# Front of an encoder kernel: S5 vectors loaded first, dummy products, squares after the input, first state products one projection later, one tile pool for three phases

## The chip, the cores and the metric

The kernel runs on one NeuronCore of a Trainium2 chip, in one launch. The metric is the device time of one execution in microseconds (us), from which three runs of the kernel before are shown below; the profiled execution is a further one.

## The reference

A trunk of two layers over 512 positions of width 1024, all in fp32. What matters here is layer 0, whose first stage is changed most:

```
h = rms_norm(x, g)                               # over the 1024 features
z = h @ w_in                                     # 1024 x 2048: q, k, v, u (512 columns each)
a = neighbourhood_attention(q, k, v, rpb)        # 8 heads of 64
lam_bar = exp(lam * exp(log_dt))                 # S5: 2 directions, 32 groups, 64 complex states
b_bar   = ((lam_bar - 1) / lam) * B
state_t = lam_bar * state_(t-1) + b_bar @ u_t    # forwards and backwards
y = u * d + sum over directions of Re(C @ state)
x = x + concat(a, glu(gelu(y))) @ w_out
```

After it, in both layers, come a gated MLP with a convolution of width 3 over the positions ("ffn", 2816 hidden features, two halves), a gated per-layer input ("ple"), and in layer 1 a retention mixer in place of the above; a last RMSNorm ends it.

## The kernel before

**Tiles.** Positions lie on the free axis: a tile is 128 features x 512 positions, and x is eight such tiles. Every projection (`proj`, L139 to L143 with `mm3`) makes 128 output features: eight weight blocks of 128x128, each with three matmuls of 128x512, since a number is carried as a rounded high part and a low rest: low weights x high x (L141), high x high (L142), high weights x low x (L143). That is 24 matmuls a projection in layer 0. `split` makes the two parts of x (high on ScalarE L177, low on VectorE L178).

**Weights.** They come in chunks c0, c1, c2 ... of eight blocks, in the order of use: chunks c0 to c3 are the four u projections, c4 to c7 are q0 to q3, c8 to c11 are k0 to k3. SyncE (SP) fetches a chunk into `wr` (three buffers), ScalarE rounds it to `wh` (L113), and VectorE subtracts to `wl` (L121, from c4 on L123). For chunks c6 to c15 `wl` is -`wr` on ScalarE (L118), onto which a DMA issued by GpSimd (POOL) adds the weights again from HBM (L119). `wh` and `wl` have four buffers each, so a chunk's split waits until the projection four before it has read its own.

**Stage one** (`mixer0`). On ScalarE and VectorE the order up to `region.close()` is that of the code; on TensorE (PE) and elsewhere a scheduler places what the code writes. `prep_small` queues the small S5 vectors (dt, magnitude, angle, powers of lam_bar: 128x32 and the like) as a list, from which `do(n)` emits n at a time between the splits of x; they read `svec`. Each x tile is also squared (L209) and the squares are added to one tile on VectorE; four products with a column of ones (L241, in `Rstd`) sum it over the partitions, and POOL and VectorE make r = 1/rms of it (128x4). `spread` turns r into a row over all partitions with four PE transposes (L252) and a ScalarE copy (L255).

The projections of u and q need no r; what reads them multiplies by the row: `u_out` (L563) scales u on VectorE, writes it to HBM (`u_scr`, L566), and reads it back in another order as `U` (L567). The input tables of S5 are made by `prep_w1` for table q of eight (three VectorE operations for each of a real and an imaginary part, on p1r, p1i and the b tables, 128x512), and turned by `trans_w1` (four PE transposes each, L487, then a ScalarE copy L489). `states` multiplies a pair of tables with `U` (L591), and four pairs fill `XV`, on which the scans run (`local`, `carry`). `prep_w2` makes output tables, `prep_blk` zeroed tiles into which blocks of the b tables are copied, `strips0` a first product of b and c tables with which this stage of PE ends. The loop that ties them together (L676 to L692):

```
for n in range(8):
    prep_w1(n + 1)               # tables for the next step
    ps = proj(xg) if n else q0   # q0 to q3, then k0 to k3
    if n:
        after_trans(n - 1)       # turn table n - 1; after odd ones, states of the pair
    next_w2(W2_K[n])
```

**Later phases.** `tp` ("act") is a pool of 53 tiles of 128x512 for everything; in the ffn a second pool `fe` of 20 tiles, made anew for each ffn, takes some of the hidden layer's high and low parts (h, l), and in the retention one of 16 tiles (`rte`). They lie in space that the other phases use otherwise. In the ffn each of 22 steps makes two projections, two tiles `c` (L1008 on ScalarE, two VectorE operations each, then gelu, a product on POOL, high part on ScalarE L1018, low part on POOL).

## Time and profile before

| what | value |
|---|---|
| median of three runs | 1525.79 us (1525.31 to 1527.48) |
| profiled execution, its own time | 1527.03 us |
| its span, first to last instruction | 1525.2 us |
| mean granted TensorE clock in it | 0.991 |
| PE busy | 1495.3 us (98%) |
| VectorE (DVE) busy | 915.7 us (60%) |
| ScalarE (ACT) busy | 615.1 us (40%) |
| POOL busy | 363.9 us (24%) |

The profile's times count from the first instruction of the profiled execution; its own time is 1.8 us more than the span, and lies 1.24 us above the median. A granted clock of 1.00 is the full 2.4 GHz, 0.50 is 1.2 GHz. PE rows give a matmul's time with its overlap with the next, so what a matmul costs in a chain is the distance between two starts.

### The profile page before, as it was taken

Reading aid. Unit: us, or ns where it says so; the run is one execution under the profiler, and the core shown is the slowest. Engines: PE = TensorE matmul, PEld = TensorE weight load, DVE = VectorE, ACT = ScalarE, POOL = GpSimd, SP = SyncE. Lnnn points to the kernel's source line nnn. Section 1 sums busy time; section 2 is a strip of 40 time slices with the busy share of each in tenths; the row PEclk is TensorE's granted clock in tenths of the full one; section 3 lists DMA queues with packets and bytes.
Section 4 is the critical chain, followed back from the end, with each engine's and each line's share of the span. In section 5 each row is a group of like instructions: output and inputs, shape, how many; then the busy total and the mean of one; then the engine's idle time right before and its main releaser. Section 6 shows DMA issues by size and latency. Waiting matters only on the chain.

```text
span 1525.2 us, 18170 instructions
## 1 busy us (share of the span) xinstructions
PE 1495.3 (98%) x7152; PEld 1234.6 (81%) x7152; DVE 915.7 (60%) x1225; ACT 615.1 (40%) x859; POOL 363.9 (24%) x256
## 2 busy tenths in 40 slices
PE   7899999999999999999999999999999999999998
PEld 5687788888888888887888888888888888888887
DVE  8778966877676523485454544534467676743346
ACT  6344755544444322343434232422244444432233
POOL 0100001233232212063141231413122222212105
PEclk9799999999999999999999999999999999999999
DMA  5854392333333433333222222213333333333331
GB/s 198 219 111 141 102 255 61 94 107 97 98 96 98 120 93 93 120 126 108 72 70 84 68 84 69 83 56 97 97 97 97 97 97 97 97 97 96 97 125 56
DMA packets 58934, 158.95 MB, mean 104 GB/s; under 512 B 11744, under 2 KB 15968, under 8 KB 58848
## 3 DMA queue, kind: packets, MB, share of 16 engines
q1 hardware_dynamic: 57408, 152.55, 32.9%
q0 software_dynamic: 1440, 5.24, 2.1%
q8 instruction: 56, 0.92, 0.2%
q14 instruction: 30, 0.25, 0.1%
HBM read 149.94 MB, written 7.83 MB: 103 GB/s over the span
## 4 chain that ended last, share of the span: by engine, by line
PE 84%; DVE 7%; issue 6%; DMA 1%; POOL 1%; ACT 1%; SPq 0%; DVEq 0%; POOLq 0%; ACTq 0%
PE ps L141 27%; PE ps L143 27%; PE ps L142 27%; DVE t L168 4%; PE ps L591 1%; PE ps L926 1%; DMA t<-in_xp_dram 1%; DVE wl L123 1%; DVE t L277 1%; DVE t L774 0%; PE ps L816 0%; PE ps L241 0%; PE ps L487 0%; POOL t L175 0%; DMA vecs<-in_vec_dram 0%
## 5 line engine op out<-in xcount | busy, mean ns | idle before, releaser
L141 PE MATMUL ps<-t,wl 128*128 128x512 f32 x1568 | 615.9, 393 | 11.3 <-DVE wl L551 6.8
L142 PE MATMUL ps<-t,wh 128*128 128x512 f32 x1568 | 611.8, 390 | 0.0
L143 PE MATMUL ps<-t,wh 128*128 128x512 f32 x1568 | 608.8, 390 | 0.7 <-DVE t L277 0.7
L113 ACT ACTIVATE wh<-wr 128x1024 fp32r<-128x1024 f32 x241 | 254.4, 1059 | 556.2 <-PE ps L143 277.5
L123 DVE TENSOR_TENSOR wl<-wr,wh 128x1024 fp32r<-128x1024 f32 x228 | 298.2, 1309 | 288.9 <-ACT wh L113 288.8
L141 PEld LDWEIGHTS ps<-t,wl 128*128 128x128 f32 x1568 | 296.2, 189 | 75.5 <-DVE wl L551 6.8
L143 PEld LDWEIGHTS ps<-t,wh 128*128 128x128 f32 x1568 | 295.8, 189 | 64.2 <-DVE t L277 1.8
L142 PEld LDWEIGHTS ps<-t,wh 128*128 128x128 f32 x1568 | 296.3, 189 | 60.2
L168 POOL TENSOR_TENSOR t<-t,t 128x512 f32<-128x512 f32 x117 | 177.9, 1522 | 457.6 <-ACT t L1014 279.3
L168 DVE TENSOR_TENSOR t<-ps,t 128x512 f32<-128x512 f32 (+1 forms) x86 | 59.3, 698 | 114.8 <-PE ps L143 103.4
L168 DVE TENSOR_TENSOR t<-t,t 128x512 f32<-128x512 f32 (+2 forms) x113 | 96.8, 878 | 27.8 <-ACT t L200 20.7
L168 DVE TENSOR_TENSOR pad<-ps,t 128x512 f32<-128x512 f32 x88 | 60.5, 692 | 82.4 <-PE ps L143 82.4
L1010 DVE SCALAR_TENSOR_TENSOR t<-pad,vecs,t 128x512 f32<-128x512 f32 x88 | 102.3, 1164 | 1.4
L168 POOL TENSOR_TENSOR t<-t 128x512 f32<-128x512 f32 x33 | 50.3, 1527 | 190.0 <-DVE t L168 190.0
L141 PE MATMUL ps<-e,wl 128*128 128x512 f32 x216 | 85.4, 395 | 0.0
L143 PE MATMUL ps<-e,wh 128*128 128x512 f32 x216 | 85.3, 395 | 0.0
L142 PE MATMUL ps<-e,wh 128*128 128x512 f32 x216 | 85.2, 395 | 0.0
L175 POOL TENSOR_TENSOR t<-t,t 128x512 fp32r<-128x512 f32 x41 | 58.6, 1446 | 60.1 <-ACT t L174 51.5
L1011 DVE SCALAR_TENSOR_TENSOR t<-pad,vecs,t 128x512 f32<-128x512 f32 x88 | 70.0, 796 | 2.9
L1008 ACT ACTIVATE t<-pad,vecs 128x512 f32<-128x512 f32 x88 | 70.2, 802 | 3.4 <-DVE pad L168 3.4
L141 PE MATMUL ps<-wh,t 128*128 128x512 f32 x160 | 62.6, 391 | 0.0
L143 PE MATMUL ps<-wl,t 128*128 128x512 f32 x160 | 62.3, 389 | 0.0
(212 smaller groups left out, 1314.1 us busy)
## 6 DMA issues: line engine op xcount, KB each, us to landing
wr<-in_wts_dram SPq DMA_DIRECT2D x241, 512.0 KB, 3.6
wl<-in_wts_dram POOLq DMA_DIRECT2D x10, 512.0 KB, 7.5
pj_scr<-t SPq DMA_DIRECT2D x16, 256.0 KB, 5.1
t<-pj_scr SPq DMA_DIRECT2D x16, 256.0 KB, 4.1
t<-in_xp_dram SPq DMA_DIRECT2D x8, 256.0 KB, 5.3
t<-in_bias_dram SPq DMA_DIRECT2D x8, 256.0 KB, 4.1
Tm<-k_scr SPq DMA_DIRECT2D x8, 256.0 KB, 6.7
t<-in_xn_dram SPq DMA_DIRECT2D x8, 256.0 KB, 6.6
```

The costliest lines, as they stand in the source:

```text
L113: act.activation(out=h, in_=raw, func=ACTF.Copy)
L123: late.append(lambda: dve.tensor_tensor(out=l, in0=raw, in1=f(h), op=ALU.subtract))
L141: pe.matmul(out=ps, lhsT=lhs[1], rhs=rhs[0], start=start, stop=False)
L142: pe.matmul(out=ps, lhsT=lhs[0], rhs=rhs[0], start=False, stop=False)
L143: pe.matmul(out=ps, lhsT=lhs[0], rhs=rhs[1], start=False, stop=stop)
L168: eng.tensor_tensor(out=out, in0=a, in1=b, op=op)
L175: low.tensor_tensor(out=l, in0=src, in1=f(h), op=ALU.subtract)
L277: self.late.append(lambda: dve.scalar_tensor_tensor(out=l, in0=x, scalar=g, in1=f(h), op0=ALU.mult, op1=ALU.subtract))
L591: pe.matmul(out=pw[:, i, :], lhsT=w1t["ri"[c], g // 4][:, 128 * (g % 4):128 * (g % 4) + 128], rhs=U[:, g, :], start=True, stop=True)
L1008: act.activation(out=c, in_=t[:, 1:513], func=ACTF.Identity, scale=vcol(cw + 44 + j), bias=vcol(V_CB + 44 * i + j))
L1010: dve.scalar_tensor_tensor(out=c, in0=t[:, 0:512], scalar=vcol(cw + j), in1=c, op0=ALU.mult, op1=ALU.add)
L1011: dve.scalar_tensor_tensor(out=c, in0=t[:, 2:514], scalar=vcol(cw + 88 + j), in1=c, op0=ALU.mult, op1=ALU.add)
```

## The change

Seven edits, in the order in which they run:

- `svec` is the first DMA of SP, ahead of x; the first eight small vector operations stand ahead of the split of x0 (`DO_X`).
- Ten products of the ones tile with itself (128x128) stand on PE ahead of the first projection (`WARM`); nothing reads them.
- All eight splits of x come before the squares, and the weights of chunk c2 are split before them. The squares are added in pairs only, so `Rstd` sums four tiles with 16 products in place of one with four.
- Table 1 (`prep_w1(1)`) is made before r, and q1 is multiplied before `spread`.
- Tables are turned and multiplied two steps behind the projections in place of one (`after_trans(n - 2)`).
- The zeros of `prep_blk` are written by four ScalarE copies of the ones scaled by 0, not by POOL memsets.
- One pool "upper" of 20 tiles, opened past the first mixer and kept to the end, replaces the 20 of each ffn and the 16 of the retention. It takes x, the rms row, the tiles `c` and the low parts of the last seven hidden tiles; the rest of h and l, and all of the retention's, are in `tp`. The 8 tiles `full` of the last phase come from `tp` too.

```diff
-DO_X = (0, 0, 0, 6, 6, 6, 6, 6)
+DO_X = (8, 6, 4, 6, 6, 6, 6, 6)
+WARM = 10
+UPPER = 20
...
-            parts = ss.parts()
+            parts = ss if isinstance(ss, list) else ss.parts()
...
-            self.row = T()
+            self.row = T(special=True)
...
+        svec = sp.tile([128, 96], F32, name="svec")
+        nc.sync.dma_start(out=svec, in_=vec[:, V_LRE:V_LRE + 96])
         xt = [T() for _ in range(KD)]
...
-                    pool.memset(t, 0.0)
+                    act.activation(out=t.rearrange("p (a b) -> p a b", b=128),
+                                   in_=ones.rearrange("p (a b) -> p a b", a=1).to_broadcast([128, 4, 128]),
+                                   func=ACTF.Copy, scale=0.0)
...
+        wm = PS()
+        for _ in range(WARM):
+            pe.matmul(out=wm[:, 0:128], lhsT=ones, rhs=ones, start=True, stop=True)
         prep_small()
         for k in range(KD):
+            do(DO_X[k])
             xg.append(split(xt[k], scale=nvec[:, k:k + 1]))
-            do(DO_X[k])
...
-            if k >= SQ_LAG:
-                ss.add(xt[k - SQ_LAG], sq=True)
-        for k in range(KD - SQ_LAG, KD):
-            ss.add(xt[k], sq=True)
+        w_split(2)
+        squares = []
+
+        def square(k):
+            t = T()
+            act.activation(out=t, in_=xt[k], func=ACTF.Square)
+            if k % 2:
+                tt(dve, squares[-1], squares[-1], t, ALU.add)
+            else:
+                squares.append(t)
+
+        for k in range(4):
+            square(k)
...
         w_split(3)
+        for k in range(4, KD):
+            square(k)
         do(99)
...
-        st_ = Rstd(ss, D)
-        q0 = proj(xg)
+        prep_w1(1, "r")
+        prep_w1(1, "i")
+        st_ = Rstd(squares, D)
+        ready = [proj(xg), proj(xg)]
         st_.spread()
...
-            if n < 7:
-                prep_w1(n + 1, "r")
-                prep_w1(n + 1, "i")
+            if n < 6:
+                prep_w1(n + 2, "r")
+                prep_w1(n + 2, "i")
...
-            ps = proj(xg) if n else q0
+            ps = ready.pop(0) if ready else proj(xg)
...
-            if n:
-                after_trans(n - 1)
+            if n > 1:
+                after_trans(n - 2)
             next_w2(W2_K[n])
+        after_trans(6)
         after_trans(7)
...
+        upper[0] = ctx.enter_context(tc.tile_pool(name="upper", bufs=UPPER))
...
-        extra[0] = ph.enter_context(tc.tile_pool(name=f"fe{i}", bufs=20))
...
-                c = T()
+                c = T(special=True)
...
-            use = m < 10
-            h, l = T(F32R, special=use), T(F32R, special=use)
+            h, l = T(F32R), T(F32R, special=m >= KF - 7)
...
-        extra[0] = ph.enter_context(tc.tile_pool(name="rte", bufs=16))
...
-                    ys[4 * h + e] = split(sg[e], low=pool, special=4 * h + e < 7)
+                    ys[4 * h + e] = split(sg[e], low=pool, special=4 * h + e < 0)
```

On PE, between the sums of squares and the second pair of state products, the kernel before has these rows (the projections' rows, 24 for each of q0, q1 and q2, are left out; ps_552/ps_559 turn table 0, ps_630/ps_637 table 1):

```order
L241 MATMUL ps_426<-ones,t_163 128x1 x4
...
L252 MATMUL ps_471<-idn,r_431 128x128 x4
...
L487 MATMUL ps_552<-idn,t_352 128x128 x4
L487 MATMUL ps_559<-idn,t_388 128x128 x4
...
L487 MATMUL ps_630<-idn,t_496 128x128 x4
L487 MATMUL ps_637<-idn,t_501 128x128 x4
L591 MATMUL ps_644<-U,t_557 128x64 x4
L591 MATMUL ps_644<-U,t_635 128x64 x4
L591 MATMUL ps_655<-U,t_564 128x64 x4
L591 MATMUL ps_655<-U,t_642 128x64 x4
```

The changed kernel has these rows on PE from the end of the 16 sums on (left out are q0 and q1 ahead of the spread, q2 and q3 ahead of the turns, and k0 ahead of the last two rows, which turn table 2; t_434 and t_439 are table 1):

```order
L243 MATMUL ps_444<-ones,t_281 128x1
...
L254 MATMUL ps_533<-idn,r_461 128x128 x4
...
L491 MATMUL ps_646<-idn,t_360 128x128 x4
L491 MATMUL ps_653<-idn,t_396 128x128 x4
...
L491 MATMUL ps_704<-idn,t_434 128x128 x4
L491 MATMUL ps_711<-idn,t_439 128x128 x4
L610 MATMUL ps_718<-U,t_651 128x64 x4
L610 MATMUL ps_729<-U,t_658 128x64 x4
...
L491 MATMUL ps_789<-idn,t_558 128x128 x4
L491 MATMUL ps_796<-idn,t_563 128x128 x4
```

The spread has moved behind q1, and the first state products behind q3 in place of q2; only the products with table 0 stand there, those with table 1 follow behind k0.

On DVE, around the operation that reads the sums of squares (v), the kernel before makes table 1 behind the four scaled u (t_478 to t_490) and the sign change of a c table (t_118):

```order
L245 TENSOR_SCALAR v_432<-ps_426 128x4
L168 TENSOR_TENSOR v_432<-v_432,r_431 128x4 x2
...
L168 TENSOR_TENSOR t_478<-ps_287,t_476 128x512
...
L331 TENSOR_SCALAR t_118<-t_118 128x512
L168 TENSOR_TENSOR t_496<-p1r,t_312 128x512
...
L168 TENSOR_TENSOR t_496<-t_496,t_497 128x512
...
L168 TENSOR_TENSOR t_501<-t_501,t_502 128x512
```

The changed kernel has there (t_434 and t_439 are table 1, t_540 the first scaled u, t_118 the sign change, t_558 table 2):

```order
L170 TENSOR_TENSOR t_434<-p1r,t_320 128x512
L170 TENSOR_TENSOR t_435<-p1i,t_325 128x512
L170 TENSOR_TENSOR t_434<-t_434,t_435 128x512
...
L170 TENSOR_TENSOR t_439<-t_439,t_440 128x512
L247 TENSOR_SCALAR v_462<-ps_444 128x4
...
L170 TENSOR_TENSOR t_540<-ps_295,t_538 128x512
...
L333 TENSOR_SCALAR t_118<-t_118 128x512
L170 TENSOR_TENSOR t_558<-p1r,t_320 128x512
```

Table 1 with its six operations has moved ahead of r, and so ahead of the scaled u.

On ACT, around the copy of the row of r, the kernel before has:

```order
L118 ACTIVATE wl_441<-wr_326 128x1024
L118 ACTIVATE wl_520<-wr_362 128x1024
L113 ACTIVATE wh_519<-wr_362 128x1024
L255 ACTIVATE t_476<-ps_471 128x512
L118 ACTIVATE wl_598<-wr_400 128x1024
L113 ACTIVATE wh_597<-wr_400 128x1024
```

The changed kernel has there:

```order
L120 ACTIVATE wl_503<-wr_370 128x1024
L120 ACTIVATE wl_614<-wr_408 128x1024
L115 ACTIVATE wh_613<-wr_408 128x1024
L257 ACTIVATE t_538<-ps_533 128x512
L120 ACTIVATE wl_672<-wr_475 128x1024
L445 ACTIVATE t_596<-ones 128x512
```

The row's copy has moved behind the split of one more chunk (wr_400 before and wr_408 now are the same chunk, c9), and the zeros stand behind it.

## Rows read from the trace of the kernel before

**Rows 1.** Waits of PE, 0 to 280 us: total, times, longest.

```profile
PE ps L141 <- DVE wl L551: 6.8, 1, 6.8
PE ps L487 <- DVE t L168: 6.2, 2, 4.3
PE ps L141 <- DVE wl L123: 1.5, 1, 1.5
```

**Rows 2.** Windows: stretch, length, busy time of each engine, clock, DMA share, GB/s.

```profile
280.00:1500.00 1220.00, 1218.39 (x5402) 1004.53 (x5401) 681.10 (x747) 450.84 (x564) 334.43 (x221) 1.00 0.31 93
```

**Rows 3.** Timeline of PE, 24 to 121 us: start, length, instruction, count, idle before.

```profile
24.51 0.50 PE L141 MATMUL ps<-t,wl 128*128 128x512 f32 x1
...
35.55 0.95 PE L241 MATMUL ps<-ones,t 128*128 128x1 f32 x8
...
61.95 1.11 PE L487 MATMUL ps<-idn,t 128*128 128x128 f32 x4 [4.33 <-DVE t L168]
64.95 1.12 PE L487 MATMUL ps<-idn,t 128*128 128x128 f32 x4 [1.90 <-DVE t L168]
66.20 7.06 PE L591 MATMUL ps<-U,t 128*128 128x64 f32 x32
73.02 0.77 PE L141 MATMUL ps<-t,wl 128*128 128x512 f32 x1
...
76.97 0.40 PE L141 MATMUL ps<-t,wl 128*128 128x512 f32 x1
...
103.97 1.90 PE L591 MATMUL ps<-U,t 128*128 128x64 f32 x16
...
120.82 0.39 PE L517 MATMUL ps<-t,t 128*128 128x128 f32 x2
```

**Rows 4.** Windows: length, then PE, PEld, DVE, ACT, POOL, clock, DMA, GB/s.

```profile
10.00:20.00 10.00, 8.27 (x23) 5.17 (x22) 9.41 (x31) 9.04 (x18) 0.00 (x0) 0.83 1.03 393
60.00:61.00 1.00, 0.00 (x0) 0.00 (x0) 1.00 (x3) 0.00 (x0) 0.00 (x0) 0.50 1.07 369
70.00:80.00 10.00, 10.00 (x39) 8.62 (x39) 3.98 (x7) 2.65 (x6) 0.00 (x0) 0.65 0.28 70
80.00:100.00 20.00, 20.00 (x118) 17.35 (x117) 15.27 (x26) 11.82 (x18) 2.58 (x3) 1.00 0.54 110
100.00:120.00 20.00, 19.40 (x135) 17.50 (x133) 18.77 (x32) 9.79 (x15) 1.73 (x2) 1.00 0.65 144
```

**Rows 5.** Timeline of DVE, 20 to 122 us.

```profile
20.20 0.75 DVE L178 SCALAR_TENSOR_TENSOR t<-t,nvec,t 128x512 fp32r<-128x512 f32 x1
...
48.51 4.06 DVE L168 TENSOR_TENSOR t<-ps,t 128x512 f32<-128x512 f32 x4 [5.52 <-ACT t L255]
52.48 2.80 DVE L331 TENSOR_SCALAR t<-t 128x512 f32<-128x512 f32 x1
...
121.24 0.69 DVE L168 TENSOR_TENSOR t<-ps,t 128x512 f32<-128x512 f32 x1 [1.87 <-PE ps L517]
```

**Rows 6.** Timeline of ACT, 47 to 53 us.

```profile
47.91 0.57 ACT L255 ACTIVATE t<-ps 128x512 f32<-128x512 f32 x1
50.87 1.06 ACT L118 ACTIVATE wl<-wr 128x1024 fp32r<-128x1024 f32 x1 [2.39 <-PE ps L141]
```

**Rows 7.** Timeline of SP, 49 to 66 us: the issues of u_scr and U.

```profile
49.62 3.29 SPq L566 DMA_DIRECT2D u_scr<-t  x4
...
61.90 4.22 SPq L567 DMA_DIRECT2D U<-u_scr  x4
```

**Rows 8.** The tile U: its DMAs from issue to landing.

```profile
DMA to landing us min/median/max: 4.2/6.5/8.9
```

**Rows 9.** Timeline of POOL, 52 to 55 us, and of ACT and POOL, 442 to 456 us.

```profile
52.75 2.25 POOL L443 MEMSET t<- 128x512 f32 x4
...
442.95 0.80 ACT L1008 ACTIVATE t<-pad,vecs 128x512 f32<-128x512 f32 x1
...
454.00 1.81 POOL L168 TENSOR_TENSOR t<-t,t 128x512 fp32r<-128x512 f32 x1 [1.29 <-ACT t L1018]
```

More of the change, by code (lines that the diff above doesn't have):

```diff
@@ L74, in trunk_kernel @@
     seq = [0]
-    extra = [None]
+    upper = [None]
     def T(dt=F32, shape=(128, 512), special=False):
         seq[0] += 1
-        if special and extra[0] is not None:
-            return extra[0].tile(list(shape), dt, name=f"e{seq[0]}", tag="e")
+        if special and upper[0] is not None:
+            return upper[0].tile(list(shape), dt, name=f"e{seq[0]}", tag="e")
         return tp.tile(list(shape), dt, name=f"t{seq[0]}", tag="t")
@@ L170, in split @@
     def split(src, scale=None, low=None, special=False):
-        h, l = T(F32R, special=special), T(F32R, special=special)
+        h, l = T(F32R), T(F32R, special=special)
         low = low or dve
@@ L270, in push @@
             if self.key == "fin":
-                act.activation(out=self.full[:, k], in_=x, func=ACTF.Copy, scale=vcol(V_NORM["fin"] + k))
+                act.activation(out=self.full[k], in_=x, func=ACTF.Copy, scale=vcol(V_NORM["fin"] + k))
             else:
@@ L301, in mixer0 @@
         nc.sync.dma_start(out=raws[0][:, 512:1024], in_=wts[0][:, 512:1024])
-        svec = sp.tile([128, 96], F32, name="svec")
-        nc.sync.dma_start(out=svec, in_=vec[:, V_LRE:V_LRE + 96])
         for k in range(2, KD):
@@ L532, in toeplitz @@
                 nc.sync.dma_start(out=Tm[j::8], in_=ks[:, :, 16 * (7 - j):16 * (7 - j) + 128])
-        ss = SumSq(dve)
         xg = []
@@ L974, in mixer0 @@
             ps = proj(mix5)
-            x = T()
+            x = T(special=True)
             tt(dve, x, ps, xr[n], ALU.add)
@@ L1024, in ffn @@
             ps = proj(hid)
-            x = T()
+            x = T(special=True)
             tt(dve, x, ps, cur.x[n], ALU.add)
@@ L1028, in ffn @@
         hid.clear()
-        extra[0] = None
         ph.close()
@@ L1037, in ple @@
         if key == "fin":
-            nx.full = ph.enter_context(tc.tile_pool(name="fin", bufs=1)).tile([128, KD, 512], F32, name="full")
+            nx.full = [T() for _ in range(KD)]
         prj = []
@@ L1056, in finish @@
             tt(pool if n < PLE_POOL else dve, t, t, prj[n], ALU.mult)
-            x = T()
+            x = T(special=True)
             tt(dve, x, t, cur.x[n], ALU.add)
@@ L1093, in gate @@
                 mm3(pss[hh][:, 0:256], ws[k], (cur.xg[k][0][:, cut[hh]], cur.xg[k][1][:, cut[hh]]), k == 0, k == KD - 1)
-        xl, sq = nx.full[:, KD - 1], T()
+        xl, sq = nx.full[KD - 1], T()
         va = nrm.tile([128, 4], F32, name="va", tag="r")
@@ L1115, in turn @@
                     pe.transpose(out=turned[j, k // 4][:, 128 * (k % 4):128 * (k % 4) + 128],
-                                 in_=nx.full[:, k, 128 * j:128 * j + 128], identity=idn)
+                                 in_=nx.full[k][:, 128 * j:128 * j + 128], identity=idn)
         def value(hh):
@@ L1257, in retention @@
             done = gated(h, sg, ss)
-        extra[0] = None
         ph.close()
@@ L1266, in retention @@
                 mm3(ps, weights(), ys[k], k == 0, k == 15)
-            x = T()
+            x = T(special=True)
             tt(dve, x, ps, cur.x[n], ALU.add)
```

## The prediction

> **What bounds the kernel now.** I read the waits of PE first. PE is busy for 98% of the span, so only its idle time, its slow time and added work can change the end by much. In the 1220 us from 280 to 1500 PE is idle for 1220 - 1218.39 = 1.6 us, at clock 1.00 [rows 2]. The reader is to see in this one row that the later phases, where the new pool and the moved tiles act, can win about 2 us at the most, and can lose without a limit, since PE has no reserve there. The waits before 280 us lie at the start (6.8 us for the first low weights), ahead of q0 (1.5 us, low weights of c4) and ahead of the turns of table 1 (6.2 us in two waits) [rows 1].
>
> The third of these is the place to read. In the timeline of PE the turns of table 1 begin at 61.95 after 4.33 us of standing, and at 64.95 after 1.90 us; then come the first state products at 66.20, and k0 at 73.02 [rows 3]. The releaser is DVE, which made table 1 only behind the four scaled u (48.51, 4.06 us) and a sign change that took 2.80 us [rows 5]. The four scaled u themselves waited 5.52 us for ACT's copy of the row. The clock belongs to this wait: PE stood from 61.95 - 4.33 = 57.62, and at 60 to 61 us the granted clock is 0.50, the level of 1.2 GHz [rows 4]. The 32 rows of state products then take 7.06 us, where the 16 at 103.97 take 1.90, so 3.80 for 32 [rows 3]. Nine matmuls of k0 pass from 73.02 to 76.97, 0.439 us each; a full-clock stretch is 24.51 to 35.55, 48 matmuls in 11.04, 0.230 each.
>
> **The change part by part.** The sum is on PE's path up to the end of the stage, at 120.82 + 0.23 = 121.05 [rows 3].
>
> Start. The ten dummy products lie in the 6.8 us in which PE waits anyway [rows 1]. Four transposes of the same shape take 1.11 us at half clock [rows 3]; ten products at twice that each are 5.6 us, below 6.8, so they cost nothing; without that cover they would cost these 5.6. The svec DMA ahead of x and small operations ahead of the first split can delay the first matmul; I bound that by one issue slot, 0.5 us, an estimate. What PE can win: u2 begins at 24.51 [rows 3]. u0 and u1 can't end before the last low part of x, which before ends at 20.20 + 0.75 = 20.95 [rows 5] and which I expect within 1 us of that, since the adds of squares that leave its way are replaced by small operations and by weight splits. So the gain lies between -0.5 and 24.5 - 22.3 = 2.2. How much, depends on the clock, whose mean is 0.83 from 10 to 20 us while PE is busy for 8.27 of 10 and DVE for 9.41 [rows 4]: PE waits there for what DVE and ACT hand it. I take 0.8.
>
> The Trainium skill says in "TensorE: Matmul & The Clock Gate", Part 1, that the array's default is the throttled rate and that activity releases it. By that the dummy products alone would bring the whole 2.2; the row shows PE fed too slowly for a good part of the stretch, and the sum goes by 0.8.
>
> Sums of squares. Four products take 0.95 us at 35.55 (eight rows, since each is two in the trace) [rows 3]. Sixteen are 3.2 to 3.8; I take 3.2, the later ones overlapping, so 2.4 more. It lies on the path. The wait of 1.5 us for the low weights of c4 [rows 1] goes: DVE has three adds fewer ahead of them, and PE comes 2.4 later. So q0 begins at 24.51 - 0.8 + 11.04 + 3.2 = 37.95, where it began before (35.55 + 0.95 + 1.50 = 38.00). These edits cancel.
>
> Tables, lag and spread. Table 1 is made ahead of r, so both DVE waits of PE, 4.33 + 1.90 = 6.23 us, go, as long as DVE makes it before 63; it is there some 12 us earlier, six operations (0.69 each at most, 4.1) before r, which has q1's 5.5 us to hide in. If PE no longer stands, the clock stays at full: 7.06 - 3.80 = 3.26 on the state products, 3.95 - 9 x 0.230 = 1.88 on k0, and half of the two turns' 2.23 is 1.1 [rows 3]. Together 6.23 + 3.26 + 1.88 + 1.1 = **12.5 us**. One projection more (q3, 5.5) stands ahead of the states; it is moved, not added.
>
> U. What takes over is U. The row's copy now stands behind q1 and behind chunk c9's split. That split waits for PE until 50.87 [rows 6]; two splits of 1.06 and 1.05 follow, and the copy (0.57) ends at 53.5, 5.0 later than before (47.91 + 0.57 = 48.48). Before, the first scaled u began at 48.51, its round trip let the first U be issued at 61.90 [rows 7], and it landed 4.2 later at the earliest [rows 8]: 66.1, 17.6 us from start to landing. PE now wants it after q0 to q2 (57.62 - 38.00 = 19.6 before), q3 (5.5) and the turns (1.1, half of 2.23): at 37.95 + 26.2 = 64.1. With the old round trip U comes at 53.5 + 17.6 = 71.1, a stall of 7.0. With uncrowded queues it comes after one scaled u (4.06 / 4 = 1.0), and two trips of 4.2: 53.5 + 9.4 = 62.9, no stall. In the old run the DMA share was 1.07 in this stretch [rows 4], with chunk loads and the accumulating loads of c7 to c9 in the queues. u_scr now starts 5.0 us later against these loads: c7 and c8 hang on u3, q0 and the raw buffers of c4 and c5, all no later than before, and c12's load goes ahead of u_scr rather than between its writes and U. So much of that traffic should be over at 54, and I stay near the light end: 65.1, a stall of **1.0**.
>
> DVE. It is the other candidate. From 48.51 to the end of its tables at 121.24 - 1.87 = 119.37 it has 70.9 us; its idle time there is 6.0, 4.7 and 0.6 (10 - 3.98, 20 - 15.27, and 20 - 18.77 less the last 0.63) [rows 4], so 59.5 us of work. Six operations moved away take 3.6 (0.6 each as they overlap). The sign change took 2.80 beside POOL's memsets [rows 5, 9]; with these gone it should be near the 0.69 of a like operation, 2.1 less (bounds 0 and 2.1). DVE would end at 53.5 + 59.5 - 3.6 - 2.1 = 107.3, PE at 121.05 - 12.5 + 1.0 = 109.5. DVE has 2 us to spare, and without the 2.1 just none. The zeros cost ACT four writes near 0.57, in idle time behind the row's copy.
>
> Later phases. The state scans and attention behind 121 us follow DVE and PE, which both move by about 11.5; I let them shift as a block. In the ffn a tile `c` is alive from 442.95 to 454.00 + 1.81 = 455.81, 12.9 us [rows 9], and two are needed in every 48 matmuls (11.0), so at most three at once. Of 20 tiles eight hold x, one the row and up to seven the low parts: four are left. So I put the pool at 0, with -2 as the best case.
>
> **Sum.** -12.5 + 1.0 = -11.5. On the profiled execution that is 1527.0 - 11.5 = 1515.5; on the median 1525.8 - 11.5 = 1514.3.
>
> **The rivals.**
> 1. U is late. Its round trip remains 17.6 us, since u_scr is written and read in small pieces behind the same loads. PE stands for 7.0 in place of 6.23, and the clock falls again: the gain is 12.5 - 7.0 = 5.5 with a kept clock, and 5.5 - 3.26 - 1.88 = 0.4 without it. That gives 1520.3 to 1525.4; in the middle 1522.5. For it: the DMA share of 1.07. Against: the loads of c7 and c8 start no later, while u_scr starts 5.0 us later.
>
> The skill's page of the same name, section "Why this matters for your kernels", says that idle gaps of PE between bursts of matmuls bring the half rate back. The rows at 57.62 to 61 agree; by it rival 1 ends near 1525.4, not 1520.3.
>
> 2. The gain is taken back behind 121 us, because attention waits for something that does not move, as a DMA queue or ACT. Then 1524 to 1527. Against: nothing in the waits of PE up to 280 us names a DMA.
> 3. It becomes slower through the upper pool. If a tile `c` of the last seven ffn steps gets its place late, ACT waits with it, PE's sums stay unread and PE stands. It decides from 11.5 + 3 = 14.5 us on, that is 1.0 us a step in 14 steps of two ffn's. Half a projection, 2.8 us a step, is 39 us, and with the gain 1553. For it: four free places for three tiles is close, and PE has 1.6 us of idle in 1220. Against: 12.9 us of life and 11.0 of period fit in four places with 9 us over.
> 4. More than the sum: the start brings its 2.2, U stalls nothing, and the pool wins 2: 1525.8 - 12.5 - 1.4 - 2 = 1510.
>
> **How the numbers follow.** The sum with its bounds (stall 0 to 3, start 1.3 worse to 1.4 better, pool 2 better) holds 1510.9 to 1517.6 and has 0.60; rival 4 and beyond 0.07; rival 1 0.18 (two thirds of it below 1522.7); rival 2 0.08; rival 3 0.07. The range 1509 to 1522 leaves out the two last cases, a third of rival 1 and some of rival 4. What a measurement of this kernel can tell from no change is about 0.2%, 3.05 us, so faster means below 1522.7: 0.60 + 0.07 + 0.12 = 0.79; same 0.06 + 0.07 = 0.13; slower 0.08.
>
> **What would show it.** Right: PE stands at the first state products for at most 3 us, the granted clock is 1.00 from 60 to 77 us, the sign change takes about 0.7, the sums about 3.2, and the last product of the stage ends at 108 to 110. Wrong: U landing at 70 or later, a clock of 0.50 at the state products, DVE's tables ending after PE's last product, or new waits of DVE or ACT in the ffn behind 450 us.

## The result and the profile after

The changed kernel takes 1514.31 us in the median of four runs (1511.46 to 1515.28), the kernel before 1526.63 (1525.31 to 1528.38): ratio 0.9916, with a 95% interval of 0.9897 to 0.9934, so 12.3 us less. The profiled execution took 1513.49 us, with a span of 1511.7 and a mean clock of 0.995; against that of before it is 13.5 us shorter.

The waits of PE from 0 to 280 us, which answer to [rows 1]: the two waits ahead of the turns of table 1 and the one ahead of q0 are gone, and one for U is new.

```profile
PE ps L610 <- DMA U<-u_scr: 2.6, 1, 2.6
PE ps L143 <- DVE wl L557: 1.9, 1, 1.9
PE ps L143 <- ACT t L860: 1.5, 1, 1.5
PE ps L549 <- DVE ones L320: 1.1, 1, 1.1
```

The timeline of PE up to the end of the first stage, which answers to [rows 3]:

```profile
1.06 4.63 PE L549 MATMUL ps<-ones 128*128 128x128 f32 x20 [1.06 <-DVE ones L320]
7.56 0.80 PE L143 MATMUL ps<-t,wl 128*128 128x512 f32 x1 [1.86 <-DVE wl L557]
8.15 0.63 PE L144 MATMUL ps<-t,wh 128*128 128x512 f32 x1
8.58 0.63 PE L145 MATMUL ps<-t,wh 128*128 128x512 f32 x1
...
33.93 3.63 PE L243 MATMUL ps<-ones,t 128*128 128x1 f32 x32
37.41 0.49 PE L143 MATMUL ps<-t,wl 128*128 128x512 f32 x1
...
62.27 1.03 PE L491 MATMUL ps<-idn,t 128*128 128x128 f32 x8
65.93 3.65 PE L610 MATMUL ps<-U,t 128*128 128x64 f32 x16 [2.63 <-DMA U<-u_scr]
69.34 0.77 PE L143 MATMUL ps<-t,wl 128*128 128x512 f32 x1
...
72.05 0.44 PE L143 MATMUL ps<-t,wl 128*128 128x512 f32 x1
...
85.24 1.90 PE L610 MATMUL ps<-U,t 128*128 128x64 f32 x16
...
111.83 0.44 PE L521 MATMUL ps<-t,t 128*128 128x128 f32 x2
```

The last product of the stage stands at 111.83, where it stood at 120.82: 9.0 us of the 13.5. The state products start at 65.93, hardly before those of the kernel before (66.20), but q3 is behind them by then. They wait for U, and then run slowly: 16 rows take 3.65 here and 1.90 at 85.24.

Windows of the changed kernel (columns as in [rows 4]), for the clock at that place, and for the later phases, which answer to [rows 2]:

```profile
60.00:70.00 10.00, 7.37 (x37) 6.62 (x36) 9.83 (x21) 4.67 (x12) 0.85 (x1) 0.77 1.07 206
66.00:67.00 1.00, 1.00 (x5) 1.00 (x6) 1.00 (x3) 1.00 (x3) 0.00 (x0) 0.50 1.52 207
70.00:71.00 1.00, 1.00 (x4) 0.81 (x3) 1.00 (x3) 0.00 (x0) 0.00 (x0) 0.50 1.16 321
280.00:1500.00 1220.00, 1217.35 (x5442) 1009.38 (x5441) 684.37 (x753) 453.15 (x572) 340.04 (x226) 1.00 0.31 93
```

In the last row PE's idle time is 2.65 us, 1 us more than before. The two rows do not hold the same work, since the changed kernel is 8.9 us further on at 280 us and 13.9 us at 1500, as the table of the lead below shows; its work of these 1220 us took the kernel before 5.1 us longer. PE is not less idle there, it is faster.

The timeline of DVE, which answers to [rows 5]; the sign change is at 56.23, the end of the tables at 106.30:

```profile
52.27 4.04 DVE L170 TENSOR_TENSOR t<-ps,t 128x512 f32<-128x512 f32 x4 [7.27 <-ACT t L257]
56.23 0.42 DVE L333 TENSOR_SCALAR t<-t 128x512 f32<-128x512 f32 x1
...
106.30 2.49 DVE L170 TENSOR_TENSOR t<-t,t 128x512 f32<-128x512 f32 x4
112.31 0.69 DVE L170 TENSOR_TENSOR t<-ps,t 128x512 f32<-128x512 f32 x1 [3.52 <-PE ps L521]
```

The copy of the row in the timeline of ACT [rows 6]:

```profile
51.67 0.57 ACT L257 ACTIVATE t<-ps 128x512 f32<-128x512 f32 x1
```

The issues of u_scr and U in the timeline of SP [rows 7]:

```profile
53.37 3.29 SPq L581 DMA_DIRECT2D u_scr<-t  x4
60.26 5.24 SPq L582 DMA_DIRECT2D U<-u_scr  x4
```

The landing of the tile U [rows 8], no longer than 7.5 us where the longest was 8.9:

```profile
DMA to landing us min/median/max: 5.5/6.1/7.5
```

Where the gain arises can be read by matching the matmuls of the two traces one by one, from the end backwards, since the later phases issue the same ones. The lead of the changed kernel, in us, at times of the kernel before:

```
at 210 to 512   8.86     first stage done, no change in the first half of the ffn
at 633          10.51    grew through the second projections of ffn 0
at 700 to 996   10.84
at 1096         12.20    grew through the retention's output projection
at 1116 to 1338 12.27
at 1458         13.92    grew through the second projections of ffn 1
```

So there are two gains: some 9 us in the first stage, and some 5 us in three stretches of projections in each of which PE waited for less than 1 us in either kernel. The second was in no term of the sum.

### The profile page after: what moved, and what is told of

It is laid out like the page before. It is cut to its first block, busy times and chain, and to the rows that moved or that the text cites. A ratio compares the mean times of both kernels' runs of the same rounds, so it can differ in the third digit from the quotient of the medians.

```text
span 1511.7 us, 18286 instructions
## 1 busy us (share of the span) xinstructions
PE 1491.7 (99%) x7196; PEld 1238.6 (82%) x7196; DVE 907.3 (60%) x1222; ACT 616.2 (41%) x863; POOL 361.7 (24%) x252
## 4 chain that ended last, share of the span: by engine, by line
PE 87%; issue 5%; DVE 5%; DMA 1%; ACT 1%; POOL 1%; SPq 0%; DVEq 0%; POOLq 0%; ACTq 0%
PE ps L143 28%; PE ps L145 27%; PE ps L144 27%; DVE t L170 2%; PE ps L610 1%; PE ps L946 1%; DVE wl L125 1%; DVE e L170 1%; PE ps L243 1%; DVE t L794 0%; DMA u_scr<-t 0%; DMA wr<-in_wts_dram 0%; PE ps L836 0%; DMA U<-u_scr 0%; PE ps L491 0%
## 5 line engine op out<-in xcount | busy, mean ns | idle before, releaser
L143 PE MATMUL ps<-t,wl 128*128 128x512 f32 x1784 | 698.8, 392 | 3.9 <-DVE wl L557 1.9
L144 PE MATMUL ps<-t,wh 128*128 128x512 f32 x1784 | 694.5, 389 | 0.0
L145 PE MATMUL ps<-t,wh 128*128 128x512 f32 x1672 | 649.6, 390 | 1.1 <-DVE t L279 0.9
L144 PEld LDWEIGHTS ps<-t,wh 128*128 128x128 f32 x1784 | 336.6, 189 | 68.3
L145 PEld LDWEIGHTS ps<-t,wh 128*128 128x128 f32 x1672 | 315.0, 188 | 68.6 <-DVE t L180 2.2
L170 POOL TENSOR_TENSOR e<-e,e 128x512 f32<-128x512 f32 x44 | 58.6, 1331 | 278.9 <-ACT e L1034 278.9
L170 POOL TENSOR_TENSOR t<-t,t 128x512 f32<-128x512 f32 x49 | 77.3, 1580 | 142.8 <-DVE t L170 128.0
L170 DVE TENSOR_TENSOR pad<-ps,e 128x512 f32<-128x512 f32 x88 | 60.5, 692 | 82.7 <-PE ps L145 82.7
L1030 DVE SCALAR_TENSOR_TENSOR e<-pad,vecs,e 128x512 f32<-128x512 f32 x88 | 101.4, 1154 | 2.3
L170 POOL TENSOR_TENSOR t<-e 128x512 f32<-128x512 f32 x33 | 47.5, 1442 | 183.3 <-DVE e L170 183.3
L1031 DVE SCALAR_TENSOR_TENSOR e<-pad,vecs,e 128x512 f32<-128x512 f32 x88 | 70.0, 796 | 2.9
L1028 ACT ACTIVATE e<-pad,vecs 128x512 f32<-128x512 f32 x88 | 70.2, 802 | 3.3 <-DVE pad L170 3.3
L143 PE MATMUL ps<-wh,t 128*128 128x512 f32 x160 | 62.6, 391 | 0.0
L144 PE MATMUL ps<-wh,t 128*128 128x512 f32 x160 | 62.3, 389 | 0.0
```

The costliest lines, as they stand in the source:

```text
L143: pe.matmul(out=ps, lhsT=lhs[1], rhs=rhs[0], start=start, stop=False)
L144: pe.matmul(out=ps, lhsT=lhs[0], rhs=rhs[0], start=False, stop=False)
L145: pe.matmul(out=ps, lhsT=lhs[0], rhs=rhs[1], start=False, stop=stop)
L170: eng.tensor_tensor(out=out, in0=a, in1=b, op=op)
L1028: act.activation(out=c, in_=t[:, 1:513], func=ACTF.Identity, scale=vcol(cw + 44 + j), bias=vcol(V_CB + 44 * i + j))
L1030: dve.scalar_tensor_tensor(out=c, in0=t[:, 0:512], scalar=vcol(cw + j), in1=c, op0=ALU.mult, op1=ALU.add)
```

## The experiments

All times are compared with the kernel before, run in the same session; ratios have their 95% intervals.

**The pool alone.** The kernel before with `UPPER` and all the moves of tiles, and nothing else:

```diff
+        upper[0] = ctx.enter_context(tc.tile_pool(name="upper", bufs=UPPER))
...
-        extra[0] = ph.enter_context(tc.tile_pool(name=f"fe{i}", bufs=20))
...
-            use = m < 10
-            h, l = T(F32R, special=use), T(F32R, special=use)
+            h, l = T(F32R), T(F32R, special=m >= KF - 7)
```

> The kernel before with the upper pool alone (and the tiles that the change puts in it). Theory (place of the tiles): in the trace of before, 648 matmuls of 128x512 read tiles of the ffn's and retention's extra pools and start 233.06 to 233.42 ns apart, where those on other tiles start 226.67 apart; in the changed kernel all are at about 226.7. That is 648 x 6.4 ns = 4.1 us: 1526.6 - 4.1 = 1522.5, and the pace of 226.7 in the ffn's second projections. Rival A (the forecast, the pool is worth nothing): 1526.6 within 0.5. Rival B (tiles c late): slower than before, with waits of ACT or DVE for tiles in the ffn.

Measured: ratio 0.9968 (0.9954 to 0.9982), 4.9 us faster, 2.8 to 7.0 by the interval. The forecast's zero is outside. The lead over the kernel before grows by 5.0 us from 270 to 1458 us, in the same three stretches: 4.1 of it is the price of the 648 matmuls, the rest, of which 0.3 comes between 633 and 700 us, stays open.

**The first stage alone.** The changed kernel with the pools of before:

```diff
-        upper[0] = ctx.enter_context(tc.tile_pool(name="upper", bufs=UPPER))
...
+        extra[0] = ph.enter_context(tc.tile_pool(name=f"fe{i}", bufs=20))
```

> The changed kernel with the pools of the kernel before: only the edits of the first stage. Theory: the first stage gives what the traces show at 222 us, 8.9 us, so 1526.6 - 8.9 = 1517.7, and the pool the rest. Rival (the forecast: the first stage gives all, 11.5 to 12.3): 1514.3 to 1515.1.

Measured: 0.9936 (0.9911 to 0.9961), 9.8 us faster, 6.0 to 13.6 by the interval, which holds the 8.9 of the traces and the 11.5 of the forecast alike. The lead is the same 5.18 to 5.20 us from 210 to 1498 us in its profiled execution (the longest of its four, 1522.8, with the clock at 0.50 in more places of the first stage): the later phases give nothing without the pool. With the run before, the two parts make up the whole: 4.9 + 9.8 = 14.7 against 12.3, inside their intervals.

**The kernel before, its extra tiles moved by 128 and 224 bytes.** An unused tile, ahead of each extra pool:

```diff
+        sp.tile([128, 32], F32, name="shift")
         extra[0] = ph.enter_context(tc.tile_pool(name=f"fe{i}", bufs=20))
...
+        sp.tile([128, 56], F32, name="shift")
         extra[0] = ph.enter_context(tc.tile_pool(name="rte", bufs=16))
```

> The kernel before with its own pools; one unused tile of 128 bytes a partition ahead of each ffn's extra pool and one of 224 ahead of the retention's, so that the extra tiles begin at the same place modulo 256 bytes (224) as those of the general pool, as they do in the upper pool. No instruction is added, removed or moved in code. Theory (the start within 256 bytes makes the pace): the 648 matmuls go from 233.1 to about 226.7 ns, 1526.6 - 4.1 = 1522.5. Rival A (it is which pool, or which neighbours, a tile has): no change, 1526.6, pace 233. Rival B (the two pools of the change spare waits): no change here and none seen in the waits.

Measured: 0.9963 (0.9951 to 0.9975), 5.6 us faster (3.8 to 7.5). The groups by line of the kernel before (columns: busy us, mean ns of one, with its overlap, then idle before):

```profile
L141 PE MATMUL ps<-e,wl 128*128 128x512 f32 x216 | 85.4, 395 | 0.0
L142 PE MATMUL ps<-e,wh 128*128 128x512 f32 x216 | 85.2, 395 | 0.0
L143 PE MATMUL ps<-e,wh 128*128 128x512 f32 x216 | 85.3, 395 | 0.0
```

The same of the moved one:

```profile
L141 PE MATMUL ps<-e,wl 128*128 128x512 f32 x216 | 84.1, 389 | 0.0
L142 PE MATMUL ps<-e,wh 128*128 128x512 f32 x216 | 84.0, 389 | 0.0
L143 PE MATMUL ps<-e,wh 128*128 128x512 f32 x216 | 84.0, 389 | 0.0
```

The reader is to see 395 become 389 in all three groups, which are all 648 matmuls on tiles `e`. The distance between starts goes from 233.1 to 226.7 ns, and the lead over the kernel before grows by 4.7 us from 512 to 1458 us. That rules out both rivals: no pool was merged, and the tiles of a pool kept their order.

This run is of use for the first stage too, which is that of the kernel before, unchanged. There the sign change happened to run ahead of the memsets, and took 0.41, in the timeline of DVE:

```profile
50.96 0.41 DVE L331 TENSOR_SCALAR t<-t 128x512 f32<-128x512 f32 x1
```

The timeline of PE of the same run:

```profile
61.06 0.80 PE L487 MATMUL ps<-idn,t 128*128 128x128 f32 x4 [2.36 <-DVE t L168]
66.93 7.06 PE L591 MATMUL ps<-U,t 128*128 128x64 f32 x32 [5.07 <-DMA U<-u_scr]
```

DVE kept PE waiting less, and the state products began at 66.93 and not earlier, since they waited 5.07 us for U. The kernel before has the same in its own rows: its first part of U, issued at 61.90 [rows 7], landed 4.2 us later [rows 8], at 66.1, and the products began at 66.20. U was due no sooner than DVE's tables there: the 6.23 us were not to be won by the tables alone.

**The state products later.** The changed kernel, with the products a projection behind the turns:

```diff
+        def after_states(q):
             if q % 2 == 1:
...
             if n > 1:
                 after_trans(n - 2)
+            if n > 2:
+                after_states(n - 3)
             next_w2(W2_K[n])
+        after_states(5)
         after_trans(6)
         after_trans(7)
+        after_states(7)
```

> The changed kernel with the state products one projection later (behind k0), the turns of the tables as they are. Theory (U is late by 2.63 us and brings the clock down for 6.8 us): the wait of PE for U goes, PE is at clock 1.00 from 60 to 80 us; the gain is 2.63 + half of 6.8 = 6.0 at most, 1508.3; DVE, which idled 3.5 us at the end of the stage in the changed kernel, leaves 3.5 of it, 1510.8. I expect 1509 to 1511. Rival A (the clock falls for another reason, the turns or the sums): 1514.3 - 2.6 = 1511.7 with 0.50 still there. Rival B (DVE or the scans behind bound the stage): no change, 1514.3.

Measured: 1507.53 us, 0.9861 (0.9841 to 0.9882): 0.0055 below the changed kernel, some 8 us, and with the last run below the fastest kernel here. The timeline of PE:

```profile
65.91 1.03 PE L491 MATMUL ps<-idn,t 128*128 128x128 f32 x8
66.78 3.68 PE L610 MATMUL ps<-U,t 128*128 128x64 f32 x32
```

Its windows at that place:

```profile
60.00:70.00 10.00, 10.00 (x68) 8.99 (x66) 9.79 (x21) 7.85 (x14) 1.72 (x2) 1.00 1.11 244
70.00:80.00 10.00, 10.00 (x52) 8.40 (x51) 10.00 (x18) 4.81 (x8) 0.86 (x1) 1.00 0.64 157
```

All 32 rows take 3.68 without a wait, at clock 1.00, where the 16 of the changed kernel took 3.65. This execution alone would not show why, since it is the shortest of its four (1503.78; the others took 1507.18 to 1508.65) and its clock falls nowhere ahead of its last 4 us. The other profiles do. In all seven with the new first stage in which PE waited for U, by 2.5 to 3.6 us, the clock falls to 0.50 in that wait or within 2 us of its end. (In some of them the view names DVE as the releaser; U's first part landed 0.1 us ahead of the products in each.) In the two with later state products PE doesn't wait there, and the clock is 1.00; the second is the last run below, whose clock was low at q0. So the wait for U brought the low clock at this place, and not the turns or the sums.

The time is below the 1509 to 1511 that I expected, and the 8 us are above the 6.0 that I had put as the limit, but with an interval of about 4 to 13 this shows nothing against it. The traces fit the limit: the turns of table 0 stand at 53.23, where the changed kernel has them at 55.92, ahead of anything that the edit moves on PE, and q0 ran at full clock in this execution. From these turns to the last product of the stage, at 103.27, it takes 50.0 us where the changed kernel takes 55.9. Nearly all of these 5.9 us are the wait of 2.63 and the 3.1 that the low clock cost.

**Starts of tiles, measured by themselves.** A kernel of matmuls alone: nothing of the trunk is computed.

```
names = "abcdefgh"
xs = [sp.tile([128, 520], F32R, name="x" + c) for c in names]
ws = [sp.tile([128, 264], F32R, name="w" + c) for c in names]
...
pe.matmul(out=ps, lhsT=w[:, o:o + 128], rhs=x[:, 0:512], start=k == 0, stop=k == n - 1)
```

> Not the trunk: 1584 matmuls of 128x512 alone, back to back, 24 for each pair of eight moving tiles (xa to xh) and eight weight tiles (wa to wh), each of which begins 32 bytes further modulo 256 (160, 192, 224, 0, 32, 64, 96, 128); the output is a copy of weights. Theory (the start of the moving tile within 256 bytes makes the pace): xc (224) at 0.227 us a matmul, xg (96) and xd (0) at 0.233, as the tiles of these starts in the trunk, whatever the weights' start. Rival A (the distance between the moving tile's and the weights' start): the fast pairs lie on a diagonal. Rival B (it needs the other engines' traffic): one pace for all 64 pairs.

Measured, ns from start to start in the mean of 24, worked out from the starts in its trace (rows: the weights' start modulo 256, columns: the moving tile's):

```
          160    192    224      0     32     64     96    128
w 160   227.4  233.5  229.4  233.8  233.3  234.1  233.5  233.2
w 192   233.1  227.7  233.5  229.4  233.8  233.3  234.1  233.4
w 224   233.2  233.2  227.7  233.5  229.4  233.8  233.3  234.0
w 0     234.2  232.9  232.9  226.9  233.5  229.4  233.8  233.4
```

The other four rows go on in the same way. My theory, the moving tile's start by itself, falls: every start is fast with one start of the weights, its own. Rival A holds. The groups by line for the weights that begin at 224, where xc begins at 224, xe at 32:

```profile
L86 PE MATMUL ps<-xh,wc 128*128 128x512 f32 x24 | 5.8, 396 | 0.0
L86 PE MATMUL ps<-xd,wc 128*128 128x512 f32 x24 | 5.8, 395 | 0.0
L86 PE MATMUL ps<-xg,wc 128*128 128x512 f32 x24 | 5.8, 395 | 0.0
L86 PE MATMUL ps<-xe,wc 128*128 128x512 f32 x24 | 5.7, 392 | 0.0
L86 PE MATMUL ps<-xc,wc 128*128 128x512 f32 x24 | 5.6, 390 | 0.0
```

No other engine moved data in these stretches, so the price needs no traffic.

**Tiles moved on, and tiles and weights moved on.** Two builds of the changed kernel; the first has the 128 bytes ahead of the general pool, the second ahead of the weights' pools:

```diff
+    gap = ctx.enter_context(tc.tile_pool(name="gap", bufs=1))
+    gap.tile([128, 32], F32, name="gap")
     tp = ctx.enter_context(tc.tile_pool(name="act", bufs=NT))
```

```diff
+    gap = ctx.enter_context(tc.tile_pool(name="gap", bufs=1))
+    gap.tile([128, 32], F32, name="gap")
     wraw = ctx.enter_context(tc.tile_pool(name="wraw", bufs=RAW_BUFS))
```

> The changed kernel with one unused tile of 128 bytes a partition ahead of the general pool, so that all of its tiles and those of the upper pool begin at 96 modulo 256 in place of 224; the weights stay at 224. Theory (the start of the moving tile makes the pace): about 5200 matmuls of 128x512 that read such a tile as the moving side go from 226.7 to 233.1 ns, 5200 x 6.4 = 33 us slower: 1547 in the changed kernel's terms. Rival (it is a property of the extra pools, not of the start): 1514.3, pace 226.7.

> The changed kernel with one unused tile of 128 bytes a partition ahead of the weight pools, so that weights and tiles both begin at 96 modulo 256 in place of 224. Theory after the sweep of starts (the pace is 227 where moving tile and weights begin at the same place within 256 bytes, 229 where the moving one is 64 on, 233 else): no change, 1514.3 to 1516, pace 226.7. Rival (the moving tile's own start, the theory before the sweep): as the run with the tiles alone moved on, some 30 us slower, pace 233.

Measured: the tiles alone 1.0118 (1.0103 to 1.0133), slower than the kernel before and some 31 us slower than the changed one; both together 0.9905 (0.9891 to 0.9920), as the changed kernel. The first of the groups by line of the kernel with the tiles alone moved:

```profile
L145 PE MATMUL ps<-t,wl 128*128 128x512 f32 x1784 | 708.6, 397 | 4.5 <-DVE wl L559 1.8 <-ACT t L862 1.5 <-ACT t L181 0.7
```

The same group with tiles and weights moved:

```profile
L145 PE MATMUL ps<-t,wl 128*128 128x512 f32 x1784 | 698.3, 391 | 4.5 <-DVE wl L559 2.3 <-ACT t L862 1.5 <-ACT Tm L516 0.3
```

In the trunk, too, it is the difference of the two starts that counts. Why a different start costs time, no run here shows.

**Without the dummy products.**

```diff
-        wm = PS()
-        for _ in range(WARM):
-            pe.matmul(out=wm[:, 0:128], lhsT=ones, rhs=ones, start=True, stop=True)
```

> The changed kernel without the ten dummy products. Theory (PE waits for DVE and ACT in the first 16 us, so the products bring a part of the 1.6 us by which u2 begins earlier): 0 to 1.6 slower than the changed kernel, 1514.3 to 1515.9, its first matmuls spaced 0.43 as they are with the products. Rival (they keep the clock up behind 15 us): up to 1.7 more, 1516 to 1517.6, with a half clock between 9 and 19 us that the changed kernel's profile does not have.

Measured: 0.9904 (0.9887 to 0.9920), the changed kernel's time within the intervals. The products give nothing that these runs can tell.

**One sum of squares.**

```diff
-            if k % 2:
+            if k:
                 tt(dve, squares[-1], squares[-1], t, ALU.add)
```

> The changed kernel with all eight squares added to one tile (seven adds on DVE in place of four), so that four products sum it in place of sixteen. Theory (the twelve more products lie on PE's path, 3.63 us against 0.95): 2.7 faster than the changed kernel, 1511.6; DVE's three adds of 0.6 fit into the 3 us by which the low weights of c4 are ready early. Rival A (q0 then waits for those weights again, as before the change): 0.5 to 1 faster, with a wait of 1.5 to 2 ahead of q0. Rival B (U is late by that much more): no change.

Measured: 0.9930 (0.9913 to 0.9947), 2.1 us more than the changed kernel by the ratios, an interval that meets its; in any case not 2.7 less. The timeline of PE:

```profile
33.85 0.95 PE L243 MATMUL ps<-ones,t 128*128 128x1 f32 x8
37.36 0.79 PE L143 MATMUL ps<-t,wl 128*128 128x512 f32 x1 [2.56 <-DVE wl L125]
```

q0 begins at 37.41 behind the sixteen products, and at 37.36 behind the four and the wait. The wait is there because DVE now makes the low weights of c4 later, with three more adds ahead of them. In the timeline of DVE of the changed kernel they end at 33.39 + 1.22 = 34.61:

```profile
33.39 1.22 DVE L125 TENSOR_TENSOR wl<-wr,wh 128x1024 fp32r<-128x1024 f32 x1
```

With one sum they end at 37.31:

```profile
36.09 1.22 DVE L125 TENSOR_TENSOR wl<-wr,wh 128x1024 fp32r<-128x1024 f32 x1
```

So the twelve products on PE stand in for adds on DVE that keep PE waiting as long. The wait is the one of rival A, without its gain.

**Zeros on POOL again.**

```diff
-                    act.activation(out=t.rearrange("p (a b) -> p a b", b=128),
-                                   in_=ones.rearrange("p (a b) -> p a b", a=1).to_broadcast([128, 4, 128]),
-                                   func=ACTF.Copy, scale=0.0)
+                    pool.memset(t, 0.0)
```

> The changed kernel with the zeros of the block tables written by POOL memsets again. Theory (the memsets slow DVE, but DVE has 3.5 us to spare at the end of the stage): the sign change goes from 0.42 to about 2.8 if the memsets run beside it, and the time does not change, 1514.3 within 1. Rival (DVE's tables are late for PE by then): 1 to 2.4 slower.

Measured: 0.9902 (0.9881 to 0.9924), no change. The memsets ran from 49.81 to 52.06, ahead of the sign change at 54.42, which took 0.41. So this run doesn't test the collision; it shows that the edit was not needed for the gain. In the pool alone, too, the sign change (51.95, 0.43) ended ahead of the memsets, and products for the tables ran beside them. They took 0.69 to 0.70, as elsewhere; the first of them and the memsets, in the timelines of DVE and POOL:

```profile
52.28 0.69 DVE L169 TENSOR_TENSOR t<-p1r,t 128x512 f32<-128x512 f32 x1
52.71 2.25 POOL L444 MEMSET t<- 128x512 f32 x4
```

If the memsets slowed the sign change of the kernel before, they do not slow every operation of DVE.

**The state products later, with one sum and without the dummies.** The edits of three runs above together.

> The run with the state products one projection later, with one sum as well and without the dummy products. Theory (each lies on the path by itself): 2.7 faster than the state products later alone, which were at 0.9861 of before; 0.9861 - 0.0018 = 0.984, 1503 to 1506. Rival (DVE bounds the stage now, it was busy without a gap from 50 to 100 us): 0.986, no gain from the sum, as DVE only starts on time and ends as late.

Measured: 1507.61 us, 0.9867 (0.9852 to 0.9882), no gain from the sum, as the rival had it. Its reason is not shown: in the profiled execution DVE does not start on time. The scaled u begin at 53.27, where they begin at 49.59 in the profile of the state products later, since PE waits 2.56 for the low weights of c4 ahead of q0, as above, and the clock is 0.50 from 36.3 to 43.1. From the scaled u on, DVE is busy without a gap in both, for 53.2 us, and then waits 0.94 for PE's last product: DVE and PE end the stage nearly together. The state products in the timeline of PE, and the window at that place:

```profile
70.47 3.68 PE L607 MATMUL ps<-U,t 128*128 128x64 f32 x32
70.00:80.00 10.00, 10.00 (x67) 8.97 (x66) 9.91 (x20) 5.81 (x11) 0.86 (x1) 1.00 1.00 262
```

## Why the prediction was right, and where it was right by luck

The sum said 11.5 us and 1514.3; measured were 12.3 and 1514.31. Two errors stand against each other in it. In the profiled executions the first stage gave 9.0 and not 11.5, and the later phases some 5 and not 0. The second is shown by runs, the first by one pair of executions: the first stage alone, with the same code, led by 5.2 in its profiled execution and by 9.8 (6.0 to 13.6) in its runs, so the runs by themselves do not tell 9.0 from 11.5.

Of the prediction's own signs, PE's stand at the state products (2.63), the sign change and the sums came about as it says. Two did not: the last product stands at 111.83 and not at 108 to 110, and the clock of 0.50 at the state products is one of its signs of being wrong.

- **Start: inside its bounds, at twice what was taken.** The sums begin at 33.93, 1.6 us earlier than before, where 0.8 was taken from -0.5 to 2.2. The dummy products were rightly put at no cost, and rightly not at a gain: the first matmuls behind them still start 0.43 us apart (8.15, 8.58), and without them the time is the same. That distance is the one of the rows at a granted clock of 0.50, 1.2 GHz (six matmuls in 2.71 us at 69.34). The profile prints 1.00 for this stretch, but the first record of the clock in the trace is its rise at 14.1. The Trainium skill says in "TensorE: Matmul & The Clock Gate", Part 1, that activity releases the clock; here PE was active from 1.06 to 5.69, stood for 1.86 us, and the next products ran at the low rate. In the six other profiles with the dummy products the clock is recorded as 1.00 from somewhere between 3.9 and 5.9 on, and in five of them as 0.50 again from somewhere between 7.5 and 9.3, so there the release came and was lost.
- **Sums and q0: right.** q0 begins at 37.41, where 37.95 was worked out. One sum bears it out: with DVE's adds back ahead of the weights of c4, the wait is back.
- **Tables and clock: the step that was mis-sized.** Both waits of PE for table 1 are gone, as the prediction put it. But of the 3.26 + 1.88 = 5.1 us that were to come from a kept clock, about 2 came. The prediction took a stall of 1.0 for U and, with it, a kept clock. The stall was 2.63 (PE came 0.8 earlier than worked out, at 63.30, and U 0.8 later), and the clock was 0.50 behind it: 16 state rows in 3.65 rather than 1.90, and six matmuls of k0 from 69.34 to 72.05 in 2.71, where 0.23 each are 1.4. That is 1.75 + 1.3 = 3.1 us for the clock and 1.6 for the longer stall, 4.7 in all, of which the earlier q0 and the end of the stage gave about 2 back. The part of rival 1 that says a stall brings the low clock was right already at a third of its length. The Trainium skill says in "TensorE: Matmul & The Clock Gate", section "Why this matters for your kernels", that idle gaps of PE between bursts of matmuls bring the half rate back. It warns of longer gaps than the 2.63 us here, and the measurement decides; the two runs with later state products have 1.00 without the stall. The other half of the premise, that the clock stays at full where PE doesn't stand, fails in the same profile: PE did not wait from 16 us on, it ran the sums, products of one column, from 33.93 to 37.41, and the clock was 0.50 from 38.0 to 41.4. Before the change the clock fell at q0 too, there behind a wait of 1.5, so the sum doesn't suffer from it.
- **U's round trip: between the ends, nearer to the light one.** From the first scaled u at 52.27 to the state products at 65.93 it took 13.7, where 17.6 and 9.4 bounded it and 11.6 was taken. The light end took 4.2 for each of two trips; the write took 6.9 (53.37 to the issue of U at 60.26), the first part of U 5.5. The row's copy was 1.3 us earlier than worked out.
- **DVE: right.** Its tables end at 106.30 + 2.49 = 108.8 (107.3 expected), 3.5 us ahead of PE's last product. The sign change took 0.42. That memsets beside it make the 2.80 of [rows 5] is only argued: in no profile here did the two meet again, and in all eleven others the sign change took 0.41 to 0.44.
- **The pool: the term that was mis-sized most.** It was put at 0, with 2 at best, because PE's idle time in these phases was 1.6 us. That bound holds for waits alone. What the pool brought is a shorter matmul: 648 x 6.4 ns = 4.1 us, of some 5 in the traces, shown with no pool changed at all. A busy PE at clock 1.00 was read as PE at its pace. The page of before had the trace of it, 395 in the groups on `e` and 390 to 393 in those on `t`, and the prediction did not look there. Rival 3 did not come: PE's waits past 280 us are 2.6 us in all.
- **Chances.** Rival 1 came in part, and nothing of rivals 2 and 3; rival 4 came in part too, with a better start and a pool that wins more than its 2. (The middle of rival 1's 1520.3 to 1525.4 is 1522.9, not 1522.5, which changes no chance.) The forecast is as near as it is because 2.5 lost in the first stage and 4.1 won by the pool partly cancel; with the stage as forecast and the pool's real worth the sum would have been 15.6, with both as they came it is 13.2, against 13.5 between the profiled executions and 12.3 between the medians.
- **Not separated.** Without the dummy products, with one sum or with the zeros on POOL, the runs show no loss that is clear of their noise. The earlier svec and small operations, table 1 ahead of r, the spread behind q1 and the lag of two were not taken out one by one, so what each of them brings of the first stage's gain is not shown.

## What to carry to other kernels

Where PE is busy throughout, compare the distance between starts of like matmuls group by group: a few ns in the mean of one group against another are worth more than all the waits left. When a wait is removed, ask which operand is due next at that instruction in the same run; here U was as late as the tables. One projection more in between hid the tables, and it took a second to hide U. Products that look like overhead can stand in for work on another engine, and taking them out then gives a wait in their place.

## What was not expected of the hardware

In a kernel of matmuls alone, a matmul of 128x512 in fp32r starts 226.9 to 227.7 ns after the one before where the moving tile and the weights begin at the same byte modulo 256, 229 where the moving tile begins 64 bytes further, and 232 to 234 at each of the other six distances that are multiples of 32 bytes. In the trunk it is about 227 at the same byte and about 233 at the others that it has. This is worth 4.1 us there for 648 matmuls, and some 31 us for nearly all. The Trainium skill's page "TensorE: Matmul & The Clock Gate", Part 1, gives 215.7 ns for 512 columns at full clock; here the measurement decides, and no run shows a group below 226.

The granted clock fell to 0.50 at some place between 36 and 40 us in ten of the twelve profiles of the trunk, the changed kernel's (at 38) among them, but not in that of the state products later nor in that of the zeros on POOL. Executions of one kernel differ by 1.4 us (the last run) to 7.6 (the first stage alone), 3.8 for the changed kernel, and low clocks stand at other places in each profile. How much of the scatter is the clock's was not measured.
